# A two-layer encoder on one core: the Fourier projection in unfolded form, folded when it leaves PSUM

## The chip, the cores and the metric

The kernel runs on one core of one Trainium2 chip. Times are device microseconds of one execution. The kernel before was run three times: 1118.82, 1119.74 and 1119.90 us, median 1119.74 us.

The engines are called as in the profile: PE (TensorE matmul), PEld (the loading of its stationary operand), DVE (VectorE), ACT (ScalarE), POOL (GpSimd) and SP (the queue that issues the DMAs here).

## The reference

Batch 1, 512 positions, 1024 channels, two layers, all float32. One layer, cut to what matters here:

```python
h = rmsnorm(x, norm1[l])
p = h @ w_in[l]                      # columns: u (512) | q (8 x 64) | k (2 x 64) | v (2 x 64)
y_f = real(fft2(u, axes=(position, channel), norm="ortho")) @ w_fourier[l] + b_fourier[l]
q = rope(rmsnorm(q, q_norm[l])); k = rope(rmsnorm(k, k_norm[l]))
y_a = windowed_gqa(q, k, v, sink[l])                     # |i - j| <= 128, blocks of 128 queries
x = x + concat([rmsnorm(y_f), rmsnorm(y_a)]) @ w_o[l]
h = rmsnorm(x, norm2[l])
gate, val = split(dwconv3(h @ w_up[l]))                  # 2 x 2816 channels
x = x + (silu(gate) * val) @ w_down[l]
```

The real part of the two-dimensional transform is the product of cosines minus the product of sines. Cosines are even and sines odd in each index, so the 512 positions (and the 512 channels) can be folded first: entry i plus entry 512 - i (257 "even" values, 0 to 256) and entry i minus entry 512 - i (255 "odd" values).

## The kernel before

The residual stream `x` is kept transposed: 8 tiles of 128 channels x 512 positions. A float32 product is made of three matmul passes in a reduced format: each operand is split into a high part (written by ACT, line 85) and the rest (`lo`, written by DVE or POOL, lines 88 and 91), and `mm3` issues hi*hi, lo*hi and hi*lo (lines 105, 106, 107). A weight tile is loaded by a DMA on SP into one of three buffers `wraw`, and `wsplit` makes `whi` and `wlo` of it (five buffers each).

One layer, in the order of the program:

1. `col_rstd` gives the norm's factor per position as columns (`r1`); `row_rstd` turns it, with four small matmuls (line 156), into a row that stands on every partition (`rb1`).
2. The products for k and v with a part of q (`grp` 1), and then for the rest of q (`grp` 0): positions are the rows of the result, in four blocks of 128, and each block has its PSUM bank (tags `mm` three times and `av`) for eight row tiles of `w_qkv`. The factor `r1` is applied at the eviction.
3. `fold_h(k)`, eight times: `x[k]` times gain times `rb1` (DVE), folded over positions (`fold`: two columns copied by DVE at line 244, the sum and the difference of 255 columns by POOL), and split into a `slab` pair. `load_wu` loads two row tiles of the Fourier columns of `w_in` and folds each over channels in the same manner (tile `tA`).
4. `prep` makes QK-norm, RoPE and the split of k and of the pairs of q; `turn_k` and `turn_q` transpose them.
5. The Fourier projection: folded positions x folded channels, so it falls into an even and an odd part. Per row tile it has products for 128, 128 and 1 even positions with 258 columns (`pee`), and for 128 and 127 odd ones with 256 columns (`poo`).
6. `attention` for the head pairs 3, 0, 1, 2: per head four blocks of scores, a masked softmax over DVE, ACT and POOL, transposes (line 402, noted in `steps`), and the product with `vz`.
7. `stage_out` evicts and splits; then two transforms, stage 0 over positions and stage 1 over channels, with the tables `tab` (two blocks of 128 of cosine and sine) and a "tail" row for index 256; then the product with `w_fourier` (folded by `w_fold` and POOL), unfolding to `y`, and its norm.
8. The output projection: first the Fourier half (`ys`), whose matmuls are tied behind the transposes `steps[12]` to `steps[31]` of attention, then the attention half (`ya`).
9. The ConvFFN: 44 tiles of `w_up` and, twice, 8 tiles of `w_down`. In the last part of layer 0 three `load_wu` of layer 1 are already made (`nwu`).

The order in which an engine gets its instructions is made at build time: a planner goes by the order of the program and issues what its own model of time says is ready. Buffers are handed out by tag (`TEMPS`, `BANKS`), and a tile waits until a buffer of its tag is free.

Of the kernel before, what the change touches and what calls it, by code (L numbers as in the profile page):

```python
# [16 lines left out]
P = 128  # L17
D = 1024
S = 512
L = 2  # L20
# [17 lines left out]
def encoder_kernel(tc, t):  # L38
    """Residual stream kept transposed (channels on partitions, positions free).

    Every float32 product runs as three float32r passes over exact splits
    a = hi + lo:  hi*hi + lo*hi + hi*lo.  RMSNorm's per-position factor is
    applied after the product it precedes where that is possible, its gain before.
    """
# [48 lines left out]
    def split(hi, lo, src, scale=None, eng=None):  # L93
        """hi + lo = src * scale; hi has float32r's mantissa, lo the rest."""
        if scale is None:
            act(hi, src)
            tt(lo, src, f(hi), ALU.subtract, eng)
        else:
            act(hi, src, scale=scale)
            stt(lo, src, scale, f(hi), ALU.mult, ALU.subtract)  # L100

    def mm3(out, a, b, start, stop, after=None, **kw):
        """out (+)= a^T b over split operands a = (hi, lo), b = (hi, lo)."""
        with tc.issue_after(after) if after is not None else nullcontext():
            nc.tensor.matmul(out, a[0], b[0], start=start, stop=False, **kw)  # L105
            nc.tensor.matmul(out, a[1], b[0], start=False, stop=False, **kw)  # L106
            nc.tensor.matmul(out, a[0], b[1], start=False, stop=stop, **kw)  # L107
# [24 lines left out]
    def rsqrt(ssq, n, inv, tag, bufs=2):  # L132
        """(ssq * inv + EPS) ** -0.5 on [P, n]: bit estimate and Newton steps."""
# [11 lines left out]
    def col_rstd(acc, inv, tag="tp"):  # L145
        """rstd per position as columns [position in block, block]."""
# [5 lines left out]
    def row_rstd(r, tag="tp"):  # L152
        """The same factors along the free axis, on every partition."""
# [7 lines left out]
    # -------------------------------------------------------------- constants  # L161
# [27 lines left out]
    # first use of the activation tables and of the tensor engine while the inputs arrive  # L189
    zero = temp(512, "sq")  # L190
    nc.vector.memset(zero, 0.0)
    warm = temp(512, "sq", F32R)
# [19 lines left out]
    def load_tables():  # L212
        for i in range(2):
            raw = wload(t["dft"][i], 512)
            th = cp.tile([P, 512], F32R, tag=f"th{i}", name=f"th{i}")
            tl = cp.tile([P, 512], F32R, tag=f"tl{i}", name=f"tl{i}")
            split(th, tl, raw)
            tab.append((th, tl))
        alt = wtile()[:1, :258]
# [3 lines left out]
    # ---------------------------------------------------------- norm of x tile  # L223
    def add_square(acc, src, first, eng=nc.gpsimd, tag="sq"):
# [7 lines left out]
    def norm_tile(k, g, acc):  # L232
        """Split x[k] * gain and add x[k]^2 to acc."""
# [8 lines left out]
    def fold(dst, src, eng):  # L242
        """src[..., 512] -> 0..256 even part, 257..511 odd part of 1..255."""
        nc.vector.tensor_copy(dst[..., 0:257:256], src[..., 0:257:256])
        tt(dst[..., 1:256], src[..., 1:256], src[..., 511:256:-1], ALU.add, eng)
        tt(dst[..., 257:512], src[..., 1:256], src[..., 511:256:-1], ALU.subtract, eng)

    def load_wu(l, kk):
        """Two row tiles of W_in's Fourier columns, folded."""
# [3 lines left out]
        out = []  # L253
        for k in range(2):
            w = temp(512, "tA")
            fold(w, raw[:, k * 512:(k + 1) * 512], nc.gpsimd)
            out.append(w)
        return out
# [4 lines left out]
    wu = {}  # L263
    for l in range(L):
        # ----------------------------------------- norm statistics, q, k, v
        r1 = col_rstd(acc, 1.0 / D)
        rb1 = row_rstd(r1)
        qraw = {}
        for grp in (1, 0):
            pq = [psum("mm" if b < 3 else "av") for b in range(NB)]  # L270
# [17 lines left out]
        # -------------------------------------- folded h for the Fourier half  # L288
        hs = {}

        def fold_h(k, eng):
            hr = temp(512, "tF")
            hf = temp(512, "tF")
            stt(hr, x[k], g1[:, l, k:k + 1], rb1, ALU.mult, ALU.mult)
            fold(hf, hr, eng)
            hs[k] = pair("slab")
            split(hs[k][:, 0, :], hs[k][:, 1, :], hf)
# [14 lines left out]
        def prep(us):  # L312
            """Normalised, rotated and split rows of the units us (head pairs, or "k")."""
# [3 lines left out]
            for i, u in enumerate(us):  # L317
                two = temp(1024, "act").rearrange("p (z b h d) -> p z b h d", z=2, **dims)
# [29 lines left out]
        def turn_q(qs, tag):  # L348
            """[hi; lo] of the pair's two heads, transposed."""
# [8 lines left out]
        def turn_k(kss):  # L358
            """[hi; hi] and [lo; lo] of each key head, transposed."""
# [10 lines left out]
        # ------------------------------------------------ banded attention  # L370
# [47 lines left out]
        # ----------------------------------------------------- Fourier mixing  # L418
        if l == 0:
            load_tables()  # L420

# [3 lines left out]

        pee = [psum(), psum(), psum("av")]
        poo = psum()
        for kk in range(KT // 2):
            if kk not in wu:
                wu[kk] = load_wu(l, kk)  # L430
            for k in (2 * kk, 2 * kk + 1):
                if k not in hs:
                    fold_h(k, nc.gpsimd)
                w = wsplit(wu[kk][k % 2])
                h = hs[k]
                st, sp_ = k == 0, k == KT - 1
                we = [z[:, 0:258] for z in w]
                wo = [z[:, 256:512] for z in w]
                for m, (c0, c1) in enumerate(((0, 128), (128, 256), (256, 257))):
                    mm3(pee[m][:c1 - c0, :258], [h[:, s, c0:c1] for s in range(2)], we, st, sp_)  # L440
                mm3(poo[:, 0:256], [h[:, s, 257:385] for s in range(2)], wo, st, sp_, skip_group_check=True)
                mm3(poo[:127, 256:512], [h[:, s, 385:512] for s in range(2)], wo, False, sp_, skip_group_check=True)
# [7 lines left out]
        def tail_out(pe, scale):  # L450
            b = tp.tile([1, 2, 258], F32R, tag="tail", name=nm("tail"), bufs=2)
# [3 lines left out]
        def stage_out(pe, po, scale):  # L455
            tiles = []
            for m in range(2):
                a = pair("slab", 514)
                n = P - m
                split(a[:, 0, :258], a[:, 1, :258], pe[m][:, :258], scale=scale)  # L460
                split(a[:n, 0, 258:514], a[:n, 1, 258:514], po[:n, m * 256:(m + 1) * 256], scale=scale)
                tiles.append(a)
            return tiles, tail_out(pe, scale)

        ue, ut = stage_out(pee, poo, 1.0)
        for stage in range(2):
            pe = [psum() for _ in range(2)]
            po = psum()
            pe.append(psum())
            for m, (c0, c1) in enumerate(((0, 128), (128, 256), (256, 257))):  # L470
                o = pe[m][:c1 - c0, :258]
                for i in range(2):
                    u2 = [ue[i][:, s, :] for s in range(2)]
                    if stage == 0:
                        mm3(o, [z[:, c0:c1] for z in u2], [z[:, 0:258] for z in tab[i]], i == 0, False)
                    else:
                        mm3(o, [z[:, c0:c1] for z in tab[i]], [z[:, 0:258] for z in u2], i == 0, False)
                for s in range(2):
                    if stage == 0:
                        nc.tensor.matmul(o, ut[:, s, c0:c1], altr, start=False, stop=s == 1)  # L480
                    else:
                        nc.tensor.matmul(o, altr[:, c0:c1], ut[:, s, :], start=False, stop=s == 1)
            for m in range(2):
                n = P - m
                o = po[:n, m * 256:(m + 1) * 256]
                for i in range(2):
                    kn = P - i
                    u2 = [ue[i][:kn, s, 258:514] for s in range(2)]
                    t2_ = [z[:kn] for z in tab[i]]
                    st = m == 0 and i == 0  # L490
                    if stage == 0:
                        mm3(o, [z[:, 1 + m * P:1 + m * P + n] for z in u2], [z[:, 256:512] for z in t2_],
                            st, i == 1, skip_group_check=True)
                    else:
                        mm3(o, [z[:, 257 + m * P:257 + m * P + n] for z in t2_], u2,
                            st, i == 1, skip_group_check=True)
# [218 lines left out]
```

## Time and profile before

| | |
|---|---|
| runs, median (lowest to highest) | 1119.74 us (1118.82 to 1119.90) |
| span of the profiled execution | 1114.8 us |
| time around that span, against the median | 4.9 us |
| busy: PE, PEld, DVE, ACT, POOL | 1067.8, 894.0, 789.6, 523.5, 329.5 us |
| mean granted PE clock | 0.986 |
| DMA | 99.66 MB, mean 89 GB/s |

The times of the runs and the profile are of different executions. The page gives one time for the profiled execution, its span from the first to the last instruction; what lies around it is known only as the difference to the median of the runs. Matmuls are pipelined, so that a busy PE need not be a PE at its peak, and matmuls and weight loads overlap. Idle time of an engine costs only where the chain that sets the end goes through it. By the busy times of each layer, layer 0 runs to about 568 us and layer 1 from there.

### The profile page before, as it was taken

The numbers are of one execution on the slowest core, as the hardware profiler recorded it, in microseconds if no ns is written. First come the engines' busy times: TensorE is split into PE (matmuls) and PEld (weight loads), VectorE is DVE, ScalarE is ACT, GpSimd is POOL, SyncE is SP. The second block draws the span as 40 slices with busy tenths as digits, with TensorE's granted clock in tenths as the row PEclk, the third lists the DMA queues.
The fourth block names the chain that finished last, engine by engine and source line by source line (L and its number), as shares of the span: only waits on it lengthen the run. The fifth ranks groups of instructions, "written<-read, shape, count | busy, mean of one in ns | idle before, by whom it ended". The sixth has DMA issues, their size and how long they took to land.

```text
span 1114.8 us, 14505 instructions
## 1 busy us (share of the span) xinstructions
PE 1067.8 (96%) x5187; PEld 894.0 (80%) x5187; DVE 789.6 (71%) x1362; ACT 523.5 (47%) x964; POOL 329.5 (30%) x370
## 2 busy tenths in 40 slices
PE   7878899999999999999997999999999999999998
PEld 6767788788888888888896878878888888888887
DVE  8998874888773377785549978477887535787732
ACT  4537763465442244543434677445554323554421
POOL 5778655311010001024207865561111000010100
PEclk9979999999999999999999999999999999999999
DMA  6312112223323323224321310223332322323241
GB/s 218 109 57 95 39 39 76 91 85 95 108 78 92 114 95 95 95 83 135 114 85 59 94 39 1 76 61 109 95 95 83 104 94 98 105 88 110 78 129 59
DMA packets 33226, 99.66 MB, mean 89 GB/s; under 512 B 3705, under 2 KB 8066, under 8 KB 33154
## 3 DMA queue, kind: packets, MB, share of 16 engines
q1 hardware_dynamic: 33154, 98.74, 28.1%
q8 instruction: 41, 0.67, 0.2%
q14 instruction: 31, 0.25, 0.1%
HBM read 96.63 MB, written 2.10 MB: 89 GB/s over the span
## 4 chain that ended last, share of the span: by engine, by line
PE 79%; DVE 14%; issue 2%; POOL 2%; ACT 1%; DMA 1%; SPq 0%; DVEq 0%; POOLq 0%; ACTq 0%
PE ps L107 25%; PE ps L105 25%; PE ps L106 25%; DVE wlo L88 3%; DVE act L91 2%; DVE act L88 2%; DVE tF L91 1%; PE ps L402 1%; DVE tA L394 1%; DVE slab L88 1%; DVE tF L88 1%; PE ps L390 1%; DVE pT L88 1%; POOL tA L88 1%; PE ps L149 1%
## 5 line engine op out<-in xcount | busy, mean ns | idle before, releaser
L85 ACT ACTIVATE whi<-wraw 128x512 fp32r<-128x512 f32 (+1 forms) x336 | 205.4, 613 | 378.6 <-PE ps L107 341.7
L88 DVE TENSOR_TENSOR wlo<-wraw,whi 128x512 fp32r<-128x512 f32 (+1 forms) x304 | 256.0, 844 | 138.3 <-ACT whi L85 136.4
L107 PE MATMUL ps<-act,whi 128*128 128x512 f32 x768 | 299.9, 391 | 4.4 <-DVE act L91 4.4
L106 PE MATMUL ps<-act,wlo 128*128 128x512 f32 x768 | 300.0, 391 | 0.0
L105 PE MATMUL ps<-act,whi 128*128 128x512 f32 x768 | 299.8, 390 | 0.0
L88 POOL TENSOR_TENSOR tF<-tF,tF 128x512 f32<-128x512 f32 x44 | 58.1, 1321 | 523.0 <-DVE tF L91 479.7
L107 PEld LDWEIGHTS ps<-act,whi 128*128 128x128 f32 x768 | 144.7, 188 | 35.9 <-DVE act L91 6.4
L105 PEld LDWEIGHTS ps<-act,whi 128*128 128x128 f32 x768 | 144.6, 188 | 30.3
L106 PEld LDWEIGHTS ps<-act,wlo 128*128 128x128 f32 x768 | 144.7, 188 | 30.0
L91 DVE SCALAR_TENSOR_TENSOR tF<-tF,pb,tF 128x511 f32<-128x511 f32 x176 | 134.0, 766 | 11.2 <-ACT tF L85 8.6
L88 DVE TENSOR_TENSOR tF<-ps,rb 128x512 f32<-128x512 f32 x104 | 70.7, 688 | 76.4 <-PE ps L107 62.0
L105 PE MATMUL ps<-slab,whi 128*128 128x512 f32 (+2 forms) x228 | 87.9, 386 | 1.3 <-ACT slab L85 1.3
L106 PE MATMUL ps<-slab,wlo 128*128 128x512 f32 (+2 forms) x228 | 85.2, 374 | 0.0
L107 PE MATMUL ps<-slab,whi 128*128 128x512 f32 (+2 forms) x228 | 84.9, 375 | 0.1
L85 ACT ACTIVATE tF<-tF,pb 128x512 f32<-128x512 f32 x88 | 71.6, 816 | 13.5 <-DVE tF L88 7.1
L88 POOL TENSOR_TENSOR wlo<-wraw,whi 128x512 fp32r<-128x512 f32 x40 | 55.1, 1379 | 47.0 <-ACT whi L85 42.7
L88 DVE TENSOR_TENSOR x<-x,ps 128x512 f32<-128x512 f32 (+1 forms) x49 | 33.0, 675 | 40.2 <-PE ps L107 40.2
L88 POOL TENSOR_TENSOR acc<-acc,sq 128x512 f32<-128x512 f32 x28 | 41.3, 1477 | 49.8 <-ACT sq L85 48.9
L106 PE MATMUL ps<-pT,wlo 128*128 128x512 f32 (+1 forms) x132 | 51.0, 386 | 0.0
L107 PE MATMUL ps<-pT,whi 128*128 128x512 f32 (+1 forms) x132 | 50.9, 385 | 0.0
L105 PE MATMUL ps<-pT,whi 128*128 128x512 f32 (+1 forms) x132 | 50.8, 385 | 0.0
L105 PEld LDWEIGHTS ps<-slab,whi 128*128 128x128 f32 x228 | 42.9, 188 | 9.1 <-ACT slab L85 1.8
(166 smaller groups left out, 1797.4 us busy)
## 6 DMA issues: line engine op xcount, KB each, us to landing
wraw<-in_w_up_dram SPq DMA_DIRECT2D x88, 512.0 KB, 3.6
wraw<-in_w_down_dram SPq DMA_DIRECT2D x32, 512.0 KB, 3.5
wraw<-in_w_o_dram SPq DMA_DIRECT2D x16, 512.0 KB, 3.6
wraw<-in_w_qkv_dram SPq DMA_DIRECT2D x16, 384.0 KB, 3.5
wraw<-in_w_down_dram SPq DMA_DIRECT2D x32, 192.0 KB, 2.4
wraw<-in_w_in_dram SPq DMA_DIRECT2D x8, 512.0 KB, 4.5
wraw<-in_w_fold_dram SPq DMA_DIRECT2D x8, 512.0 KB, 3.5
x<-in_xT_dram SPq DMA_DIRECT2D x8, 256.0 KB, 6.2
```

What stands on the lines that cost most here:

```text
L85: return nc.scalar.activation(out, in_, func, **kw)
L88: return (eng or nc.vector).tensor_tensor(out, a, b, op=op)
L91: return nc.vector.scalar_tensor_tensor(out=out, in0=a, scalar=s, in1=b, op0=op0, op1=op1)
L105: nc.tensor.matmul(out, a[0], b[0], start=start, stop=False, **kw)
L106: nc.tensor.matmul(out, a[1], b[0], start=False, stop=False, **kw)
L107: nc.tensor.matmul(out, a[0], b[1], start=False, stop=stop, **kw)
L149: nc.tensor.matmul(pt[:, 2 * b:2 * b + 2], acc[:, b * P:(b + 1) * P], ones2, start=True, stop=True)
L390: nc.tensor.matmul(sc[:, :n], qT[p][:, e, i * P:(i + 1) * P], kT[g][:, s, j0 * P:(j1 + 1) * P], start=s == 0, stop=s == 1)
L394: nc.vector.tensor_tensor_reduce(out=pr[:, :n], in0=sc[:, :n], in1=mask[:, m0:m0 + n], scale=-1.0 / math.sqrt(HD), scalar=nsink[:, l, h:h ...
L402: tr = nc.tensor.transpose(pp[:, j * P:(j + 1) * P], pr[:, j * P:(j + 1) * P], ident)
```

## The change

The projection of u is now made like those of q, k and v: the split tiles `xg` of the unfolded h are the stationary operand, 128 positions at a time, and the unfolded 512 Fourier columns of `w_in` are the moving one. It stands right behind q, k and v, ahead of `prep`. Four PSUM banks hold the four position blocks. At the eviction the channels are folded and `r1` is applied: ACT copies the 255 upper columns with the factor, and DVE makes a two-column scaling and two operations of 255 columns with one operand out of PSUM and the other read backwards. Each block is then split into an `act` pair. Positions are not folded at all: the position transform sums over four blocks of 128 positions, and for blocks 2 and 3 there are two more pairs of tables (every second column negated). `rb1`, `fold_h`, the folding of `w_in` and the first `stage_out` are gone, and so are the early loads for layer 1. The tables' odd parts are shifted by one row, so that all tiles have 128 rows, which takes more DMA issues for the tables and for `w_fold`. q's group takes the PSUM tags `sc` and `tp`. `prep` takes its scratch from `slab`, and the squares theirs from `tF`.

```diff
-    TEMPS = {"act": (1024, 8), "m4": (1024, 5), "slab": (1028, 4), "pT": (2560, 2),
-             "tA": (512, 6), "tF": (512, 6), "sq": (512, 2)}
+    TEMPS = {"act": (1024, 8), "m4": (1024, 5), "slab": (1024, 4), "pT": (2560, 2),
+             "tA": (388, 6), "tF": (512, 6)}
...
     def load_tables():
         for i in range(2):
-            raw = wload(t["dft"][i], 512)
+            raw = wtile()
+            nc.sync.dma_start(raw[:, :257], t["dft"][i, :, :257])
+            if i == 0:
+                nc.gpsimd.memset(raw[:1, 257:512], 0.0)
+            else:
+                nc.sync.dma_start(raw[:1, 257:512], t["dft"][0, P - 1:, 257:])
+            nc.sync.dma_start(raw[1:, 257:512], t["dft"][i, :P - 1, 257:])
...
+        for i in range(2):
+            two = []
+            for s, z in enumerate(tab[i]):
+                o = cp.tile([P, 512], F32R, tag=f"t{s}{i + 2}", name=f"t{s}{i + 2}")
+                act(o[:, 0::2], f(z)[:, 0::2])
+                act(o[:, 1::2], f(z)[:, 1::2], scale=-1.0)
+                two.append(o)
+            tab.append(two)
...
-    def fold(dst, src, eng):
-        nc.vector.tensor_copy(dst[..., 0:257:256], src[..., 0:257:256])
-        tt(dst[..., 1:256], src[..., 1:256], src[..., 511:256:-1], ALU.add, eng)
-        tt(dst[..., 257:512], src[..., 1:256], src[..., 511:256:-1], ALU.subtract, eng)
+    def fold(dst, src, scale):
+        up = temp(256, "tF")
+        act(up[:, :255], src[:, 257:512], scale=scale)
+        nc.vector.tensor_scalar(dst[:, 0:257:256], src[:, 0:257:256], scale, None, op0=ALU.mult)
+        stt(dst[:, 1:256], src[:, 1:256], scale, up[:, 254::-1], ALU.mult, ALU.add)
+        stt(dst[:, 257:512], src[:, 1:256], scale, up[:, 254::-1], ALU.mult, ALU.subtract)
...
-        rb1 = row_rstd(r1)
...
-            pq = [psum("mm" if b < 3 else "av") for b in range(NB)]
+            pq = [psum(("mm", "mm", "mm", "av")[b] if grp else ("sc", "sc", "tp", "tp")[b]) for b in range(NB)]
...
-        for k in range(4):
-            fold_h(k, nc.gpsimd)
+        if l == 0:
+            load_tables()
+        pu = [psum("mm" if b < 3 else "av") for b in range(NB)]
+        for kk in range(KT // 2):
+            raw = load_wu(l, kk)
+            for k in (2 * kk, 2 * kk + 1):
+                w = wsplit(raw[:, (k % 2) * 512:(k % 2 + 1) * 512])
+                for b in range(NB):
+                    mm3(pu[b], [xg[k][:, s, b * P:(b + 1) * P] for s in range(2)], w, k == 0, k == KT - 1)
+        ub = []
+        for b in range(NB):
+            uf = temp(512, "tF")
+            fold(uf, pu[b], r1[:, b:b + 1])
+            a = pair("act")
+            split(a[:, 0, :], a[:, 1, :], uf)
+            ub.append(a)
...
-                two = temp(1024, "act").rearrange("p (z b h d) -> p z b h d", z=2, **dims)
+                two = temp(1024, "slab").rearrange("p (z b h d) -> p z b h d", z=2, **dims)
...
-        ue, ut = stage_out(pee, poo, 1.0)
-        for stage in range(2):
...
+        for m, (c0, c1) in enumerate(((0, 128), (128, 256), (256, 257))):
+            for b in range(NB):
+                mm3(pe[m][:c1 - c0, :258], [ub[b][:, s, c0:c1] for s in range(2)], [z[:, 0:258] for z in tab[b]],
+                    b == 0, b == NB - 1)
+        for m in range(2):
+            for b in range(NB):
+                mm3(po[:, m * 256:(m + 1) * 256], [ub[b][:, s, 256 + m * P:384 + m * P] for s in range(2)],
+                    [z[:, 256:512] for z in tab[b]], m == 0 and b == 0, b == NB - 1, skip_group_check=True)
+        ue, ut = stage_out(pe, po, 1.0)
...
-            raw = wload(t["w_fold"][l, j], 1024)
+            raw = wtile()
+            to, fr = [z.rearrange("p (z i c) -> p z i c", z=2, i=4) for z in (raw, t["w_fold"][l, j])]
+            nc.sync.dma_start(to[:, :, 0:2], fr[:, :, 0:2])
+            nc.sync.dma_start(to[1:, :, 2:4], fr[:P - 1, :, 2:4])
+            for i in (2, 3):
+                nc.sync.dma_start(to[:1, :, i], fr[P - 1:, :, 5 - i])
...
-                    if m < 3:
-                        nwu[m] = load_wu(l + 1, m)
```

More of the change, by code (lines that the diff above doesn't have):

```diff
@@ L450, in tail_out @@
         def tail_out(pe, scale):
-            b = tp.tile([1, 2, 258], F32R, tag="tail", name=nm("tail"), bufs=2)
+            b = tp.tile([1, 2, 258], F32R, tag="tail", name=nm("tail"), bufs=1)
             split(b[:, 0, :], b[:, 1, :], pe[2][:1, :258], scale=scale)
@@ L457, in stage_out @@
             for m in range(2):
[L458 to L461, printed above, removed]
+                a = pair("slab")
+                split(a[:, 0, :257], a[:, 1, :257], pe[m][:, :257], scale=scale)
+                split(a[:, 0, 257:], a[:, 1, 257:], po[:, m * 256 + 1:(m + 1) * 256], scale=scale)
@@ L462, in stage_out @@
                 tiles.append(a)
             return tiles, tail_out(pe, scale)
-        ue, ut = stage_out(pee, poo, 1.0)
-        for stage in range(2):
[L467 to L496, printed above, removed]
-            ue, ut = stage_out(pe, po, 1.0 if stage == 0 else 1.0 / 512.0)
@@ new lines, in encoder_kernel @@
+        ue, ut = stage_out(pe, po, 1.0)
+        pe = [psum(), psum()]
+        po = psum()
+        pe.append(psum())
+        for m, (c0, c1) in enumerate(((0, 128), (128, 256), (256, 257))):
+            o = pe[m][:c1 - c0, :258]
+            for i in range(2):
+                mm3(o, [z[:, c0:c1] for z in tab[i]], [ue[i][:, s, 0:258] for s in range(2)], i == 0, False)
+            for s in range(2):
+                nc.tensor.matmul(o, altr[:, c0:c1], ut[:, s, :], start=False, stop=s == 1)
@@ L499, in encoder_kernel @@
+        for m in range(2):
+            for i in range(2):
+                mm3(po[:, m * 256:(m + 1) * 256], [z[:, 256 + m * P:384 + m * P] for z in tab[i]],
+                    [ue[i][:, s, 256:512] for s in range(2)], m == 0 and i == 0, i == 1, skip_group_check=True)
+        ue, ut = stage_out(pe, po, 1.0 / 512.0)
         accF = accum("accF")
```

52 lines of the change are left out of this document (9 added, 43 removed).

## The prediction

> **What bounds the kernel now.** I read the page of the profile first (busy shares and the 40 slices).
>
> ```profile
> span 1114.8 us, 14505 instructions
> ...
> PE 1067.8 (96%) x5187; PEld 894.0 (80%) x5187; DVE 789.6 (71%) x1362; ACT 523.5 (47%) x964; POOL 329.5 (30%) x370
> ...
> PE   7878899999999999999997999999999999999998
> DVE  8998874888773377785549978477887535787732
> ```
>
> PE is busy for 96% of the span, so PE work that is added has a price somewhere. But the second row shows PE below 9 in the first five slices (27.9 us each) and in slice 22, at the heads of the two layers, and there the third row has DVE at 7 to 9. So the 96% is an average: two long stretches (the ConvFFN) where PE alone sets the pace, and two shorter ones (the mixing half of a layer) where it is fed late. Next the windows view of the mixing halves, with q, k, v at its head (layer 0: 40 to 160 us; layer 1: 580 to 710 us). The columns are the stretch, its length, then busy time of PE, PEld, DVE, ACT, POOL, the granted clock, and the DMA.
>
> ```profile
> 40.00:50.00 10.00, 8.59 (x45) 7.31 (x43) 10.00 (x14) 1.71 (x4) 8.49 (x9) 1.00 0.41 120
> 50.00:80.00 30.00, 20.12 (x120) 18.05 (x120) 29.73 (x55) 11.35 (x22) 26.10 (x33) 0.72 0.25 78
> 80.00:100.00 20.00, 15.30 (x98) 11.81 (x96) 17.36 (x33) 11.65 (x28) 13.47 (x12) 0.91 0.18 68
> 100.00:160.00 60.00, 55.50 (x354) 47.96 (x353) 50.47 (x168) 47.88 (x131) 41.69 (x75) 1.00 0.18 60
> 580.00:630.00 50.00, 42.21 (x266) 39.45 (x264) 46.81 (x78) 24.18 (x49) 35.49 (x38) 0.93 0.17 52
> 630.00:650.00 20.00, 17.34 (x115) 13.63 (x116) 19.52 (x49) 15.06 (x39) 17.08 (x19) 1.00 0.32 103
> 650.00:710.00 60.00, 57.67 (x355) 48.63 (x356) 45.23 (x153) 44.05 (x118) 36.19 (x65) 1.00 0.12 36
> ```
>
> Between 50 and 80 us (the Fourier projection of layer 0) DVE is busy for 29.7 of 30 us and POOL for 26.1, while PE has 20.1, at a granted clock of 0.72. I count as lost the idle time of PE plus its busy time times the clock that was missing: 1.4 us in 40 to 50, 9.9 + 20.1 x 0.28 = 15.5 in 50 to 80, 4.7 + 1.4 = 6.1 in 80 to 100, 4.5 in 100 to 160; in layer 1 7.8 + 3.0 = 10.8, 2.7 and 2.3. Together 27.5 + 15.8 = 43.3 us. That is the pool from which the change can pay. The third view is the timeline of PE around the projection (start, duration, what it waited for).
>
> ```profile
> 52.51 0.58 PE L105 MATMUL ps<-whi,slab 128*128 128x258 f32 x1 [2.58 <-ACT pT L85]
> ...
> 79.91 0.28 PE L107 MATMUL ps<-wlo,slab 128*127 128x256 f32 x1
> ...
> 607.11 0.28 PE L105 MATMUL ps<-whi,slab 128*128 128x258 f32 x1
> 607.23 0.29 PE L106 MATMUL ps<-whi,slab 128*128 128x258 f32 x1
> ...
> 612.68 0.58 PE L107 MATMUL ps<-wlo,slab 128*128 128x258 f32 x1 [2.53 <-DVE wlo L88]
> ...
> 629.53 0.28 PE L107 MATMUL ps<-wlo,slab 128*127 128x256 f32 x1
> ```
>
> Starts lie 0.12 us apart while the next duration is 0.28: matmuls overlap, so I price them by the distance of their starts, not by their durations. The projection is 8 row tiles x 15 matmuls = 120, which at 0.12 is 14.4 us, but it lasts from 52.51 to 79.91 (27.4) and from 607.11 to 629.53 (22.4). The row at 612.68 says why: a low half `wlo` that DVE delivered 2.53 us late. DVE and POOL, not PE, bound this stage.
>
> **The change, part by part: PE.** Two more parts of the timeline, and one group of instructions (count over both layers | busy us, mean ns | idle before), give the prices.
>
> ```profile
> 299.81 0.39 PE L105 MATMUL ps<-act,whi 128*128 128x512 f32 x1
> 300.03 0.39 PE L106 MATMUL ps<-act,wlo 128*128 128x512 f32 x1
> 300.26 0.39 PE L107 MATMUL ps<-act,whi 128*128 128x512 f32 x1
> ...
> 581.44 1.05 PE L156 MATMUL ps<-ident,nr 128*128 128x128 f32 x8
> 582.25 0.42 PE L106 MATMUL ps<-whi,act 128*128 128x384 f32 x1
> ```
>
> ```profile
> L480 PE MATMUL ps<-altr,tail 1*128 1x258 f32 x8 | 2.0, 331 | 0.0
> ```
>
> The unfolded projection is 8 row tiles x 4 position blocks x 3 passes = 96 matmuls of 512 columns, 0.225 us apart: 21.6 us in place of 14.4, +7.2 a layer. The position transform sums over four blocks in place of two and a tail row: 3 x 2 x 3 = 18 more of 258 columns and 2 x 2 x 3 = 12 more of 256, 30 x 0.12 = 3.6, less the 6 tail matmuls; one of these costs between 0.12 (the distance above) and 0.33 (the whole duration, in the last row), and I take 0.2, in the middle: -1.2, together +2.4. The factors along the free axis, `rb1`, go: 582.25 - 581.44 = 0.8. Sum: 7.2 + 2.4 - 0.8 = +8.8 us of PE a layer, 17.6 us in all (16 to 18.6 by the bounds of the tail). It lies on the path wherever PE sets the pace.
>
> The Trainium skill, "TensorE: Matmul & The Clock Gate", section "Back-to-back issue gap", gives a sustained distance of about 131 ns for 512 columns and 81 for 128. By it the new projection would be 96 x 0.131 = 12.6 us and the old one about 120 x 0.098 = 11.8 (estimates from that page), so PE would pay some 13 us less over both layers than in my sum; the rows above, 225 ns for 512 and 120 for 258, contradict it, and the sum goes by the rows.
>
> **DVE, POOL and ACT.** The other groups:
>
> ```profile
> L91 DVE SCALAR_TENSOR_TENSOR tF<-x,pa,rb 128x512 f32<-128x512 f32 x16 | 17.2, 1074 | 1.4 <-ACT rb L85 1.3
> L244 DVE COPY tF<-tF 128x2 f32<-128x2 f32 x16 | 7.1, 442 | 0.2
> L244 DVE COPY tA<-wraw 128x2 f32<-128x2 f32 x16 | 6.9, 468 | 3.5 <-DMA wraw<-in_w_in_dram 3.5
> L88 DVE TENSOR_TENSOR slab<-tF,slab 128x512 fp32r<-128x512 f32 x40 | 30.4, 778 | 0.0
> L88 POOL TENSOR_TENSOR tF<-tF 128x255 f32<-128x255 f32 x32 | 29.4, 942 | 40.4 <-DVE tF L91 40.4
> L88 POOL TENSOR_TENSOR tA<-wraw 128x255 f32<-128x255 f32 x32 | 29.3, 945 | 17.7 <-DMA wraw<-in_w_in_dram 17.7
> L91 DVE SCALAR_TENSOR_TENSOR slab<-ps,slab 128x258 fp32r<-128x258 f32 x12 | 4.9, 412 | 0.0
> L85 ACT ACTIVATE slab<-tF 128x512 fp32r<-128x512 f32 x40 | 24.7, 631 | 23.3 <-POOL tF L88 15.7 <-PE ps L107 3.8 <-DVE tF L244 2.5
> ```
>
> Off DVE, a layer: 8 scalings of h (8.6), 16 two-column copies (7.0), 8 low halves of the folded h (8 x 0.778 = 6.2), and one eviction of five pieces (5 x 0.41 = 2.1): 23.9 us. Onto DVE: per position block a two-column scaling (at most 0.45, like L244), two folds that read PSUM (no row has a reversed second operand with a scale; the nearest, 258 columns out of PSUM with a scale, is 0.41 and I take that; the 512-column scaling, 1.07, is the upper end) and a low half (0.78): 4 x 2.05 = 8.2 us, at most 13.5. Net -16 us of DVE a layer. Off POOL: all 32 folds a layer, (29.4 + 29.3) / 2 = 29 us; one `memset` of a row comes once. ACT loses 8 x 0.63 = 5.0, a copy and five evictions, and gains 4 x 2 activations of at most 0.63, 5.0; in layer 0 the signed copies of the tables add eight strided half tiles of at most 0.63, 5 us, hidden under q's matmuls, where ACT was busy for 1.7 us of 10.
>
> What PE then waits for in the projection: a row tile takes PE 12 x 0.225 = 2.7 us, and needs 0.63 of ACT and 0.78 of DVE. DVE has 1.9 us of every 2.7 for the QK-norm and RoPE of `prep`, which today stands behind the folds. q's group also takes the PSUM tags `sc` and `tp`, so it does not wait until k's and v's banks are evicted (the idle time ahead of the projection, 2.58 us at 52.51, goes with it: its banks are free).
>
> **DMA and SP.** The W_in loads keep 512 KB; three of layer 1 no longer start in the ConvFFN's last tiles. They land in 4.5 us and one serves two row tiles, 5.4 us of PE, with three buffers: covered. The tables take five issues in place of two, and each W_fold tile four in place of one (32 in place of 8), 1 KB pieces. Everything behind them on SP is a weight load.
>
> ```profile
> wraw<-in_w_in_dram SPq DMA_DIRECT2D x8, 512.0 KB, 4.5
> ```
>
> I cost them at nothing; their cover is the stretch of attention in which W_fold is fetched early. Without it a tile would come late by a landing, for which I take that of the row, 4.5 us, and 8 x 4.5 = 36 us is the other end; nothing speaks for that, as the DMA share is 0.12 to 0.32 in these windows.
>
> **The sum.** The losses of 40 to 80 and 580 to 630 go, since their cause (DVE and POOL behind the folds) goes: 1.4 + 15.5 + 10.8 = 27.7 us. Of 80 to 100 and 630 to 650 (transforms in a row, attention not ready because q's `prep` is late) I take half, 4.4 of 8.8, as attention can now stand beside the transforms. Attention's own 4.5 + 2.3 stay. 27.7 + 4.4 - 17.6 = 14.5 us less. The profiled execution's span of 1114.8 becomes 1100.3; the median of the runs, 1119.74, lies 4.9 above that span, which I leave as it is: 1105.2 us.
>
> **The rivals.** Break-even is at 17.6 of 43.3: less than 41% recovered is a slower kernel.
> (a) Everything recovered, attention's 6.8 and the other 4.4 too: 43.3 - 17.6 = 25.7 less, 1094. For it: attention may start beside the projection's matmuls. Against: its waits are a chain over four engines, and no fold is in it.
> (b) The gain is given back at one spot: every transform matmul needs the folded blocks, so after the last projection matmul PE stands for 8.2 us of folding a layer if attention is not ready. 2 x 8.2 = 16.4 back: 1121.6, no change. Against: `prep` has the projection's 21.6 us to get done.
> (c) Slower: attention becomes bound by DVE. The folding (8.2) and two evictions (2 x 2.1) now stand in the stretch where DVE already has 50.5 of 60 us (layer 0) and 45.2 (layer 1). Free there are 9.5 and 14.8, against 12.4 that come. If in-order waiting puts all of it on the path, 24.8 us come back: 1130. It decides when the attention stretches lose over 7.2 us a layer more than the 4.5 and 2.3 of today.
> (d) PE's whole extra work on the path, because the stalls come from the order of DVE's queue and merely move: 1119.7 + 17.6 = 1137. Against: 29 us of POOL and 16 of DVE do disappear in each layer. This is what the Trainium skill's "Perfetto Trace Analysis", section "Identifying the Most-Contended Engine", would make one expect, since it says to work on the engine with the highest occupancy and this change adds to it. The windows above show that in these stages it is DVE.
>
> **How the numbers follow.** Forecast 0.52 (1097 to 1116), (a) 0.12, (b) 0.15, (c) 0.16, (d) 0.05. A measurement tells about 0.2% (2.2 us) from no change, so faster means below 1117.5 and slower above 1122. Faster: 0.51 + 0.12 + a third of (b), 0.68. Same: most of the rest of (b), 0.07. Slower: (c), (d) and a little of (b), 0.25. The range runs from 1093 (all recovered) to 1124: above it lie (d) and the larger part of (c), about 0.15, below it about 0.04.
>
> **What would show it.** Right: in the projection PE busy for the whole stretch at a granted clock of 1.0, 96 matmuls in about 22 us, no waits on `wlo`; the first transposes of attention within a few us of the projection's end; POOL's 255-column folds gone. Wrong: a gap of PE over 4 us behind the projection that ends with the low half of a folded block (b); DVE over 95% in attention with PE below 90% (c); the granted clock below 1 in it; W_fold tiles landing late. The weakest step is the half of 8.8 and that attention's loss stays as it is.

## The result, and the profile after

The changed kernel takes 1205.24 us (median of four runs, 1204.05 to 1206.41), beside 1119.28 us for the kernel before on the same chip: a ratio of 1.0775, 95% interval 1.0759 to 1.0792. That is 86 us slower; the forecast was 1105.2, between 1093 and 1124. In the experiments below, one execution of e6 (the profiled one) took 1239.61 us at a granted clock of 0.83, beside 0.97 in its others, and is left out of that run's figures.

The page after, its busy shares and three rows of the 40 slices (30.1 us each here):

```profile
span 1202.3 us, 14451 instructions
...
PE 1090.7 (91%) x5171; PEld 917.5 (76%) x5171; DVE 736.2 (61%) x1320; ACT 521.1 (43%) x960; POOL 254.4 (21%) x307
...
PE   8852986999999999999999269789999999999998
DVE  8533674388785357786447247536887733787732
...
PEclk9885997999999999999999679889999999999999
```

DVE has lost 53 us of work and POOL 75, more than the 32 and 58 that the prediction took off them, and yet PE has fallen to 5 and 2 tenths in slices 2 and 3 (counted from 0), and to 2 and 6 in slices 22 and 23. DVE is not full there either (3 and 3; 2 and 4). No engine sets the pace, which points to a wait on something that is not an engine. The chain that ended last names it in its row by line, which has one entry on SP and one on a DMA of W_fold, neither of them in the row of the page before:

```profile
PE ps L105 24%; PE ps L107 24%; PE ps L106 23%; SPq L498 5%; DMA wraw<-in_w_fold_dram 2%; PE ps L416 1%; DVE act L91 1%; POOL x L88 1%; DVE x L88 1%; DVE tA L408 1%; DVE pT L88 1%; ACT act L85 1%; PE ps L149 1%; PE ps L404 1%; ACT tA L85 1%
```

L498 is the two loads of one row each that the change adds to every W_fold tile. The timeline, engine by engine, follows one such tile from the queue to PE (layer 0; start, duration, what it waited for):

```profile
76.15 0.39 PE L106 MATMUL ps<-whi,act 128*128 128x512 f32 x1
76.38 0.39 PE L107 MATMUL ps<-wlo,act 128*128 128x512 f32 x1
```

```profile
76.47 0.59 SPq L495 DMA_DIRECT2D wraw<-in_w_fold_dram  x1
77.10 0.68 SPq L496 DMA_DIRECT2D wraw<-in_w_fold_dram  x1
77.82 7.83 SPq L498 DMA_DIRECT2D wraw<-in_w_fold_dram  x2
91.88 0.59 SPq L495 DMA_DIRECT2D wraw<-in_w_fold_dram  x1
```

```profile
91.12 0.72 POOL L88 TENSOR_TENSOR wraw<-wraw 128x256 f32<-128x256 f32 x1 [9.54 <-DMA wraw<-in_w_fold_dram]
107.30 0.72 POOL L88 TENSOR_TENSOR wraw<-wraw 128x256 f32<-128x256 f32 x1 [7.82 <-DMA wraw<-in_w_fold_dram]
```

```profile
91.88 0.63 ACT L85 ACTIVATE whi<-wraw 128x512 fp32r<-128x512 f32 x1 [14.77 <-POOL wraw L88]
108.06 0.63 ACT L85 ACTIVATE whi<-wraw 128x512 fp32r<-128x512 f32 x1 [15.54 <-POOL wraw L88]
108.59 1.18 ACT L85 ACTIVATE tF<-ps,nr 128x255 f32<-128x255 f32 x3
```

```profile
110.80 0.89 PE L105 MATMUL ps<-th,act 128*128 128x258 f32 x2 [33.16 <-ACT act L85]
```

The projection runs as forecast, a matmul every 0.23 us, and ends at 77. Then: SP issues the 127-row half of a W_fold tile (L496) at 77.10; the next two issues, L498, which are in the queue behind it, take until 85.65; the tile is complete when POOL starts on its odd half, at 91.12. The next tile's loads start only at 91.88 and are complete at 107.30, 15 us a tile. ACT, whose queue has W_fold's split *ahead* of the folding of u, waits 14.77 and 15.54 us for POOL; only at 108.59 does it copy the upper columns of u, and PE, which needs the folded u for the position transform, has stood for 33.16 us. Why the planner put W_fold first on ACT is not in the trace; that it did is.

What the 127-row half costs in the DMA engines is seen by comparing two stretches of the same tile in the windows view (the last two columns are the share of the 16 engines and GB/s):

```profile
78.00:79.50 1.50, 0.00 (x0) 0.00 (x0) 0.00 (x0) 0.00 (x0) 0.00 (x0) 1.00 0.57 173
80.00:90.00 10.00, 0.00 (x0) 0.00 (x0) 1.39 (x2) 0.00 (x0) 1.59 (x3) 0.63 0.07 23
```

The 128-row half (256 KB) flows at 173 GB/s, with a share of 0.57 over the 1.5 us. The 127-row half (254 KB) trickles at 23 GB/s with a share of 0.07, which is about one engine of sixteen (0.0625). The Trainium skill states the rule for this, which I had overlooked: "DMA: Bandwidth & Descriptors", section "Why a DMA increments its semaphore by 16 and not by 1", says that a transfer is spread over the largest number of engines up to 16 that divides the sizes of its slowest dimension, and names 127 partitions as a case of one engine. The trace agrees.

### The profile page after: what moved, and what is told of

The parts are those of the page before. It is cut to its first block, busy times and chain, and to the rows that moved or that the text cites. A ratio compares the mean times of both kernels' runs of the same rounds, so it can differ in the third digit from the quotient of the medians.

```text
span 1202.3 us, 14451 instructions
## 1 busy us (share of the span) xinstructions
PE 1090.7 (91%) x5171; PEld 917.5 (76%) x5171; DVE 736.2 (61%) x1320; ACT 521.1 (43%) x960; POOL 254.4 (21%) x307
## 3 DMA queue, kind: packets, MB, share of 16 engines
q1 hardware_dynamic: 36540, 98.74, 26.5%
## 4 chain that ended last, share of the span: by engine, by line
PE 74%; SPq 6%; DVE 5%; ACT 2%; DMA 2%; POOL 2%; issue 1%; DVEq 0%; POOLq 0%; ACTq 0%
PE ps L105 24%; PE ps L107 24%; PE ps L106 23%; SPq L498 5%; DMA wraw<-in_w_fold_dram 2%; PE ps L416 1%; DVE act L91 1%; POOL x L88 1%; DVE x L88 1%; DVE tA L408 1%; DVE pT L88 1%; ACT act L85 1%; PE ps L149 1%; PE ps L404 1%; ACT tA L85 1%
## 5 line engine op out<-in xcount | busy, mean ns | idle before, releaser
L85 ACT ACTIVATE whi<-wraw 128x512 fp32r<-128x512 f32 (+1 forms) x352 | 215.2, 614 | 489.6 <-PE ps L107 357.6
L105 PE MATMUL ps<-whi,act 128*128 128x384 f32 (+1 forms) x192 | 69.3, 363 | 3.9 <-ACT whi L85 3.9
L107 PE MATMUL ps<-wlo,act 128*128 128x384 f32 (+1 forms) x192 | 69.4, 364 | 1.7 <-DVE wlo L88 1.7
L106 PE MATMUL ps<-whi,act 128*128 128x384 f32 (+1 forms) x192 | 69.5, 362 | 1.5 <-DVE act L91 1.5
L88 POOL TENSOR_TENSOR wlo<-wraw,whi 128x512 fp32r<-128x512 f32 x40 | 52.2, 1313 | 75.6 <-ACT whi L85 75.5
L105 PE MATMUL ps<-th,act 128*128 128x258 f32 (+2 forms) x20 | 7.7, 407 | 59.6 <-ACT act L85 59.6
```

The costliest lines, as they stand in the source:

```text
L85: return nc.scalar.activation(out, in_, func, **kw)
L88: return (eng or nc.vector).tensor_tensor(out, a, b, op=op)
```

## The experiments

Five theories were put to the test. **T1**: the loads of 127 rows run on one DMA engine and the tiles come late. **T2**: the two loads of one row are slow in themselves. **T3**: the order of the queues (W_fold ahead of the folding on ACT) is the cause, however quick the loads. **T4**: the squares of the attention outputs now share the tag `tF` with what is made of W_fold's products, and hold those back. **T5**: DVE bounds attention, rival (c) of the prediction.

**e1: the changed kernel, W_fold's 127 rows loaded as 112 and 15.**

```diff
-            nc.sync.dma_start(to[1:, :, 2:4], fr[:P - 1, :, 2:4])
+            nc.sync.dma_start(to[1:113, :, 2:4], fr[:112, :, 2:4])
+            nc.sync.dma_start(to[113:, :, 2:4], fr[112:P - 1, :, 2:4])
```

> The changed kernel with one edit: the 127 rows of the odd half of a W_fold tile come as two loads, of 112 and of 15 rows. Theory T1 (the 127-row load, 254 pieces of 1 KB, is carried by one of the 16 DMA engines at about 46 ns a piece, so 11.7 us, and three such tiles stand in ACT's and POOL's queues ahead of the folding of u): the W_fold tile lands within 4 us, the gaps of PE behind the projection (33.3 and 26.6 us) go, and the time falls by 50 to 75 us, to 1130 to 1155 us. Rival T2 (the one-row loads are what is slow, since SP shows 7.2 us in the issue of the first of them): nothing changes, 1205 us. Rival T3 (the order of the queues: ACT has the split of W_fold ahead of the folding, however fast the load is): at most 10 us less.

Measured: 1143.07 us, ratio to before 1.0216 (1.0201 to 1.0231). One issue more a tile, the same bytes, and 62.2 us less, as T1 expected.

**e2: the tables' loads of 127 rows split in the same manner, too.**

> As the one before, and the 127 rows of the two tables are split into 112 and 15 too. T1: besides the W_fold gaps the waits of layer 0 before the projection (about 5 us at 46 us) go; 4 to 8 us below the kernel with only W_fold split. If the steps of the prediction other than the loads hold, this one is near 1105 us; if the prediction's rival (c) or (d) holds, 1130 to 1137 us.

Measured: 1132.40 us, ratio 1.0120 (1.0103 to 1.0137), 10.7 us less than e1, a little more than expected. The gain stands ahead of the projection: in 40 to 60 us of layer 0, PE is busy for 14.76 us at a granted clock of 0.83 in e1, and for 20.00 at 1.00 in e2. By my expectation a time of 1130 to 1137 was to mean rival (c) or (d); e5 shows that it meant neither. The SP timeline shows the last three issues of such a tile now, the 15 rows (L498) and the one-row loads (L500):

```profile
67.31 0.90 SPq L498 DMA_DIRECT2D wraw<-in_w_fold_dram  x1
68.25 1.27 SPq L500 DMA_DIRECT2D wraw<-in_w_fold_dram  x2
```

The two one-row loads are issued in 1.27 us in place of 7.83. They are quick where no load of 127 rows stands ahead of them, and e4 will say the same. T2 is out.

**e3: the kernel before, with the odd half of W_fold loaded as 127 rows and two loads of one row.**

```diff
-            raw = wload(t["w_fold"][l, j], 1024)
+            raw = wtile()
+            ...
+            nc.sync.dma_start(to[:, :, 0:2], fr[:, :, 0:2])
+            nc.sync.dma_start(to[:P - 1, :, 2:4], fr[:P - 1, :, 2:4])
+            for i in (2, 3):
+                nc.sync.dma_start(to[P - 1:, :, i], fr[P - 1:, :, i])
```

> The kernel before with one part of the change alone: the odd half of each W_fold tile comes as one load of 127 rows and two of one row, in place of one load of the whole tile. T1: each tile takes about 15 us to come, and what waits for it in order is late: 20 to 70 us slower than before, 1140 to 1190 us. T2 expects the same of the one-row loads, and the next run tells them apart. T3: at most 5 us slower.

Measured: 1164.27 us, ratio 1.0405 (1.0390 to 1.0421): 45.5 us more, with nothing else of the change.

**e4: the changed kernel, the odd half loaded as 128 rows without the shift** (the odd weights stand one row off; the one-row loads stay).

> The changed kernel with the odd half of W_fold loaded as 128 rows without the shift by one row (the weights of the odd part are thus displaced by one row); the two one-row loads stay. T1: like the run with 112 and 15 rows, 1130 to 1155 us, and the first one-row load is issued in under 1 us. T2: 1205 us, with 7 us for the first one-row issue.

Measured: 1144.54 us, ratio 1.0231 (1.0210 to 1.0251), about e1's time. The same number of issues as in the changed kernel and 2 KB more a tile, 128 rows for 127: 61 us less. The pair of one-row loads, kept as it was, is issued in 1.30 us:

```profile
64.25 1.30 SPq L498 DMA_DIRECT2D wraw<-in_w_fold_dram  x2
```

T1 is shown, from both sides; the wait for it, in the view of waits, POOL for W_fold's DMA (us, times, longest), in the kernels before, after, e2, e3 and e4:

```profile
POOL wraw L88 <- DMA wraw<-in_w_fold_dram: 3.9, 3, 2.5
```

```profile
POOL wraw L88 <- DMA wraw<-in_w_fold_dram: 72.4, 9, 10.7
```

```profile
POOL wraw L88 <- DMA wraw<-in_w_fold_dram: 6.4, 4, 3.7
```

```profile
POOL wraw L88 <- DMA wraw<-in_w_fold_dram: 53.6, 10, 10.9
```

```profile
POOL wraw L88 <- DMA wraw<-in_w_fold_dram: 7.6, 5, 2.4
```

But e2 is still 14 us slower than before. In its groups of PE instructions, two waits stand out at the end of attention, and the timeline (layer 1) shows where:

```profile
L105 PE MATMUL ps<-slab,whi 128*128 128x256 f32 x24 | 9.0, 376 | 5.1 <-ACT tF L85 5.1
L149 PE MATMUL ps<-ones,accF 128*128 128x2 f32 x16 | 3.7, 355 | 8.1 <-POOL accF L88 8.1
```

```profile
693.90 0.41 PE L417 MATMUL ps<-ident,tA 128*128 128x128 f32 x2 [0.18 <-DVE pT L88]
698.59 0.58 PE L105 MATMUL ps<-slab,whi 128*128 128x256 f32 x1 [2.56 <-ACT tF L85]
...
713.12 1.87 PE L149 MATMUL ps<-ones,accF 128*128 128x2 f32 x8 [4.09 <-POOL accF L88]
```

The last transpose of attention is at 693.90, and only behind it come the last W_fold products, their norm (713.12) and the output projection that needs it: a chain over four engines with little beside it. The clock falls with it: in 700 to 720 us PE is busy for 13.39 us at a granted clock of 0.59 (in e5, below, for 20.00 at 1.00).

Buffers go out in the program's order; there are six of `tF`, and attention's three squares come before W_fold's `u`, `y` and squares in it. The theory is that most of these get a buffer only once a square of attention has been made, added and freed. That is argued from the code; the next runs test it.

**e5: e2, with the squares' scratch from `m4` in place of `tF`.**

```diff
-            add_square(accA, py, first_pair, nc.vector if p == 2 else nc.gpsimd)
+            add_square(accA, py, first_pair, nc.vector if p == 2 else nc.gpsimd, tag="m4")
```

> The kernel with all 127-row loads split (e2_both_112), and one edit: the squares of attention's outputs take their scratch from the tag m4 in place of tF. Theory T4: a tag's buffers are handed out in the order of the program, attention stands ahead of the Fourier chain in the program, so the unfolding behind the transforms, which takes its tiles from tF too, waits until the last head pair's square has had its tF buffer; attention then runs without other matmuls, and the chain from W_fold to the norm stands alone behind it (PE gaps of 2.7, 4.1, 2.8 and 0.7 us a layer, and half of the clock). It expects W_fold's products of tiles 1 to 3 inside attention again and 20 to 35 us less: 1097 to 1112 us. Rival T5: the chain is late because DVE and ACT are bound by attention (the prediction's rival (c)); then the products stay behind attention and the time stays within 4 us of 1132.

Measured: 1099.16 us, ratio 0.9828 (0.9810 to 0.9846): one tag, 33.2 us, and 1.7% less than before. T5 is out with it, as the edit leaves DVE's work as it was. In the same two groups, and in the timeline of layer 1 (whose last transpose of attention is now at 695.34), the waits are gone and the norm stands in the middle of attention:

```profile
L105 PE MATMUL ps<-slab,whi 128*128 128x256 f32 x24 | 7.1, 297 | 0.0
L149 PE MATMUL ps<-ones,accF 128*128 128x2 f32 x16 | 1.9, 241 | 0.0
```

```profile
662.65 0.95 PE L149 MATMUL ps<-ones,accF 128*128 128x2 f32 x8
```

**e6: the kernel before, with only its squares moved to `tF`**, in the way that the change does.

> The kernel before with one part of the change alone: the squares of attention's outputs take their scratch from tF in place of the tag sq. T4: the Fourier chain falls behind attention as in the changed kernel, 15 to 35 us slower, 1134 to 1154 us. T5: within 3 us of the kernel before.

Measured: median 1157.84 us (three runs, 1154.04 to 1158.21), ratio 1.0342 (1.0316 to 1.0368). That is 39.5 us more by the medians, above the 35 that I gave as the most: T4 is shown from both sides, too. No trace of e6 is read, so that the place of its 39.5 us is not shown.

**e9: the changed kernel with the squares on `m4` alone**, its loads on one engine kept.

> The changed kernel, its one-engine loads kept, with one edit: the squares of the attention outputs take their scratch from m4 in place of tF. Two independent causes (additive): the tag is worth the 33 us that it was worth on top of the split loads, so about 1172 us. Rival, one cause hides the other (the W_fold tiles come at 75 to 120 us anyway, and the tag is what the loads make late): less than 10 us, 1195 or more. Third: the tag costs more with late loads, below 1165.

Measured: 1178.79 us, ratio 1.0538 (1.0521 to 1.0556), where independent causes had 1172. The tag is worth 26.5 us here and 33.2 on top of the loads, the loads (W_fold and tables) 72.8 alone and 79.6 on top of the tag: two causes, independent to some 7 us, neither hiding the other.

**e11: e5, with ACT's split of W_fold put behind the folding of u.** The wait of T3 was left. In the group of PE's first products of the position transform (count | busy, mean | idle before), for the kernels after, e5 and e11:

```profile
L105 PE MATMUL ps<-th,act 128*128 128x258 f32 x8 | 3.5, 483 | 59.6 <-ACT act L85 59.6
```

```profile
L105 PE MATMUL ps<-th,act 128*128 128x258 f32 x8 | 3.4, 472 | 9.3 <-ACT act L85 9.3
```

```profile
L105 PE MATMUL ps<-th,act 128*128 128x258 f32 x8 | 2.3, 315 | 1.3 <-ACT act L85 1.3
```

```diff
-            split(a[:, 0, :], a[:, 1, :], uf)
+            last = act(a[:, 0, :], uf).ins
+            tt(a[:, 1, :], uf, f(a[:, 0, :]), ALU.subtract)
...
-            w = wsplit(wf_[:, :512], nc.gpsimd)
+            with tc.issue_after(last):
+                w = wsplit(wf_[:, :512], nc.gpsimd)
```

`last` is the split of the fourth u block on ACT when W_fold's split is tied to it.

> The repaired version with ACT's splits of the W_fold tiles put behind the folding of the u blocks in ACT's queue. Theory: the 5.8 and 3.8 us that PE stands behind the projection come from ACT, which waits there for a W_fold tile that POOL has not combined; they shrink to the folding's own first block (copy 0.46, two folds 0.86, splits), some 2 to 3 us each, and 4 to 6 us go: 1093 to 1096. Rival: the time moves on to a later wait (W_fold products later, attention first): within 2 us of 1099.2. PE order differs little from the repaired version.

Measured: 1092.65 us (1091.91 to 1095.12), ratio 0.9773 (0.9756 to 0.9789), 6.5 us less than e5. ACT's queue in layer 1 before and after the tie (e5, then e11):

```profile
608.21 0.47 ACT L85 ACTIVATE tF<-ps,nr 128x255 f32<-128x255 f32 x1 [0.21 <-PE ps L107]
612.85 0.63 ACT L85 ACTIVATE whi<-wraw 128x512 fp32r<-128x512 f32 x1 [4.16 <-POOL wraw L88]
613.38 0.82 ACT L85 ACTIVATE tF<-ps,nr 128x255 f32<-128x255 f32 x2
```

```profile
607.79 0.62 ACT L85 ACTIVATE act<-tF 128x512 fp32r<-128x512 f32 x1
...
611.66 1.17 ACT L85 ACTIVATE whi<-wraw 128x512 fp32r<-128x512 f32 x2
```

In e5 the next copies of u wait until 613.38, behind a split of W_fold; in e11 the first folded block is already split at 607.79, and W_fold comes at 611.66, behind all four. T3 alone is worth those 6.5 us once the loads are quick. In the changed kernel it is what lets a late W_fold tile, wanted much later, stop the folding.

**e10: e5 with q's group back on the PSUM banks of k and v**, one step of the change undone.

> The repaired version (loads split in 112 and 15 rows, squares on m4) with q's group back on the PSUM banks of k and v (mm, av) instead of sc and tp. My prediction gave the other banks the 2.58 us that PE waited ahead of the projection in layer 0 and something like it in layer 1: 2 to 5 us more than 1099.2, so 1101 to 1104. Rival: DVE and ACT evict early enough, or the planner puts a block of q behind a free bank: within 1.5 us of it. A gap of PE of 2 to 3 us between the groups would be seen in the first case.

Measured: 1103.21 us, ratio 0.9863 (0.9847 to 0.9880), 4.0 us more. The size is that of the forecast, the place is not: PE shows no wait between the groups, and the 4 us are spread over several stretches; what of them is the banks and what another order of the planner is open.

**e7, e12, e13: W_fold laid out shifted before the launch, so that each tile is one load of 128 rows.** e7 is e5 with W_fold and the sine tables so, e12 is e5 with W_fold alone, e13 is e11 with both.

> As e5_sq_m4, but W_fold and the sine tables are laid out with the shift by one row before the launch, so that each tile is one load of 128 rows as in the kernel before. T1 says that loads of 112, 15 and 1 rows cost a little more than one load (five issues on SP of about 0.6 us in place of one of 0.3, 1 KB pieces): 0 to 6 us less than e5_sq_m4, with the time of the prediction, 1105 us, inside reach. If the split loads still held the queues, it is over 8 us less.

> The repaired version with W_fold alone laid out shifted ahead of the launch (one load of 128 rows a tile), the tables still split in their five to seven loads. With both laid out so it took 1109.0 us against 1099.2. If W_fold's eight tiles make that difference (each load of 1 KB pieces spread over all engines, no 1-row loads, hence another order by the planner): 1106 to 1111. If the tables make it: 1098 to 1100. Something else between or outside of these means that the 10 us are the spread of the planner's orders and belong to no one edit.

> The version with the folding ahead of W_fold's splits on ACT (1092.65 us), and with W_fold and the sine tables laid out shifted before the launch, so that every tile is one load of 128 rows. Without the tie on ACT the same simplification took 1109.0 in place of 1099.2. If that loss came from ACT's queue (W_fold's splits ahead of the folding, earlier still with quicker loads), the tie removes it: 1089 to 1093. If it is attention that falls into another order, it stays: 1098 to 1104.

Measured: e7 1108.98 us, ratio 0.9912 (0.9894 to 0.9931); e12 1105.01, ratio 0.9876 (0.9859 to 0.9892); e13 1091.75, ratio 0.9758 (0.9743 to 0.9773). I expected e7 to be up to 6 us better than e5, and it was 9.8 worse, with simpler loads. e12 is between the two forecasts, which by its expectation means that the 10 us belong to no one edit. e13 is 17.2 us better than e7, as expected if ACT's queue was at fault. But the wait behind the projection does not explain it all. The row of the position transform in e7, which is that of e5 over again, and in e13:

```profile
L105 PE MATMUL ps<-th,act 128*128 128x258 f32 x8 | 3.3, 439 | 9.4 <-ACT act L85 9.4
```

```profile
L105 PE MATMUL ps<-th,act 128*128 128x258 f32 x8 | 2.3, 315 | 0.8 <-ACT act L85 0.8
```

So of the 17 us the tie accounts for some 9 where it acts. Part of the rest lies in attention: in 100 to 160 and 650 to 690 us PE is busy for 54.56 and 34.69 us in e7, at granted clocks of 0.97 and 0.96, and for 56.75 and 37.61 at 1.00 in e13. That the planner's order there is the reason is argued and not shown; why e7 got the worse one was not settled. e13 is not told apart from e11 (their intervals overlap); they are the two best versions.

## Why the prediction was wrong

**The sign was lost in the sentence "I cost them at nothing".** I gave the DMA issues as an upper end 8 x 4.5 = 36 us, by the landing of a load of 128 rows, and set it aside because the DMA share was low. Both were wrong: the loads, those of the tables among them, cost 72.8 to 79.6 us, about twice that end. "W_fold tiles landing late" stands in the prediction as a sign of being wrong, but no rival and no chance went with it. The price of the wrong row: a 127-row tile takes 15 us where I took 4.5, its split in e1 alone gives back 62.2 us, and the tables', which I did not bound at all, 10.7. And a low share is no cover: 0.07 is just what one busy engine looks like.

**The second cause was never priced.** The front of this document says that the squares take theirs from `tF`; the sum has no term for it. It cost 26.5, 33.2 and 39.5 us in e9, e5 and e6. A tile whose tag changes can change the order of the work, as a moved step does, and needs a sentence on who waits for that buffer.

**The wait behind the projection, rival (b).** I named a gap of PE over 4 us behind the projection as the sign of (b), and gave it 8.2 us a layer from the folding. The gap is there, 59.6 us over both layers, but it is not the folding, which PE waits for 1.3 us in e11: the order of ACT's queue passed W_fold's lateness on.

**The rest of the sum, read in the mended kernel.** From the changed kernel it is 1205.2, less 62.2 (e1), 10.7 (e2), 33.2 (e5), 6.5 (e11) = 1092.6. That is 12.6 us under the forecast and just below its range; the tie of e11 is no part of the change, and e5, without it, is 6.0 under the forecast. The windows of e11 that answer to those of the prediction (the first three stretches and the last are cut a little otherwise; attention ends before 700 here):

```profile
40.00:80.00 40.00, 38.41 (x212) 33.29 (x211) 34.98 (x67) 20.19 (x41) 20.02 (x20) 1.00 0.33 106
80.00:100.00 20.00, 17.60 (x125) 15.04 (x125) 11.24 (x41) 14.57 (x41) 12.85 (x21) 1.00 0.36 107
100.00:160.00 60.00, 56.77 (x341) 48.40 (x340) 43.01 (x139) 40.15 (x105) 36.75 (x67) 1.00 0.15 44
...
580.00:630.00 50.00, 48.77 (x291) 42.18 (x290) 40.17 (x85) 31.20 (x68) 26.20 (x30) 1.00 0.28 86
630.00:650.00 20.00, 19.64 (x137) 17.57 (x137) 15.19 (x57) 16.38 (x46) 12.31 (x23) 1.00 0.16 47
650.00:690.00 40.00, 37.63 (x222) 32.15 (x223) 30.90 (x100) 26.39 (x71) 22.24 (x41) 1.00 0.10 31
```

Idle time of PE in them: 1.6 + 2.4 + 3.2 + 1.2 + 0.4 + 2.4 = 11.2 us, with the clock at 1.00 throughout. Of 43.3 us I had forecast 32.1 to go and 11.2 to stay. That the sums agree to a tenth is luck (the parts do not, and layer 1 runs earlier in e11, its projection ending at 608 in place of 630), but the pool was right, and so was its cause: with the folds gone from the projection, its stalls are gone too. The spans differ by 1114.8 - 1090.1 = 24.7 us, where the sum had 14.5: PE's term of 17.6 us is too high. If nothing changed outside these windows, 32.1 less 24.7 leaves 7.4 us for it. By the pages PE's busy time times its granted clock grows from 1067.8 x 0.986 = 1053 to 1065.2 x 0.999 = 1064 us, 11 and not 17.6, though a mean clock makes this rough. The new projection is as priced:

```profile
586.10 0.39 PE L105 MATMUL ps<-whi,act 128*128 128x512 f32 x1
...
607.44 0.39 PE L106 MATMUL ps<-whi,act 128*128 128x512 f32 x1
607.67 0.39 PE L107 MATMUL ps<-wlo,act 128*128 128x512 f32 x1
```

From the first to the end of the last, at 608, it takes 22 us, and the starts lie 0.23 us apart, as taken. The old one holds as well in layer 0: in 50 to 80 us PE was busy for 20.12 us at a granted clock of 0.72, or 14.5 at full clock, for the 14.4 taken. So what was sized wrong lies elsewhere, in the transforms or in how the matmuls of the mixing half overlap; no run settles which.

**The folding.** I gave a block 0.45 at most, two folds of 0.41 and a low half of 0.78. The groups of e11:

```profile
L91 DVE SCALAR_TENSOR_TENSOR tF<-ps,nr,tF 128x255 f32<-128x255 f32 x16 | 6.9, 473 | 0.0
L88 DVE TENSOR_TENSOR act<-tF,act 128x512 fp32r<-128x512 f32 x8 | 6.2, 817 | 0.0
L262 DVE TENSOR_SCALAR tF<-ps,nr 128x2 f32<-128x2 f32 x8 | 1.7, 214 | 0.8 <-ACT tF L85 0.8
```

0.21 + 2 x 0.47 + 0.82 = 2.0 us a block for 2.05: the nearest rows were good enough. What DVE lost beyond the 32 us of the sum is in part work that stayed and ran shorter: its 64 low halves of 384 columns took 46.9 us before and 37.8 after, and why is not shown. Rival (c) is out: in 100 to 160 us DVE is busy for 43.0 us of 60, less than the 50.5 of before. So is (d), as the mended kernel is faster than before. Rival (a), 1094, is the time that the change reaches when its loads, its tag and ACT's order are mended.

## What to carry to other kernels

Here a load's shape set its price, and not its bytes: before a tile is shifted by a row, look whether the number of rows is still a multiple of sixteen, as 128 and 112 are and 127 is not, and if not, split it (112 and 15) or shift the data beforehand. When a scratch tile changes its tag, write down which tiles come behind it in that ring and whether one of them is wanted earlier than it is freed. And when a stretch has *no* engine near full, ask first what the queue behind the late one was meant to do: here a tile that was wanted only later held up the one that PE stood for.

## What the runs showed of the hardware

A load of 127 rows ran at 23 GB/s, and its tile was complete 14 us after its issue (77.10 to 91.12), while one of 128 rows flowed at 173 GB/s. The queue pays, too: the two one-row issues behind it took 7.83 us on SP, and 1.30 in e4, behind a load of 128 rows. And PE pays twice for a stop. In the changed kernel's windows behind the stop of 33 us, which ends at 110.80, the granted clock is 0.50 up to 116 us, 0.76 in 124 to 130 us, after more waits, and back at 1.00 only from 130 us:

```profile
112.00:116.00 4.00, 3.69 (x17) 2.92 (x16) 3.34 (x6) 1.61 (x4) 0.69 (x1) 0.50 0.18 38
...
130.00:140.00 10.00, 9.79 (x74) 8.41 (x73) 5.89 (x23) 7.64 (x23) 4.25 (x10) 1.00 0.01 2
```
